# Recurrent half of an output projection by one Strassen step, with the bias tables moved to another pool and a plain block moved up in the attention half

## The chip, the cores and the metric

The kernel runs on one core of one Trainium2 chip. The metric is device time in microseconds (us) of one execution. TensorE is called PE, VectorE DVE, ScalarE ACT, GpSimd POOL and SyncE SP, as in the profile.

## The reference, cut to what matters

One layer of an encoder with 512 positions and model width 1024, in float32. The part around the change is this:

```python
y_rnn = (h_f + h_b) * gelu(gate)                    # (512, 512), recurrent heads
y_attn = dilated_attention(qh, kh, vh, rel_bias)    # (512, 512), 8 heads of 64
mix = concatenate([rms_norm(y_rnn, norm_rnn_g), rms_norm(y_attn, norm_attn_g)], axis=-1)
x = x + mix @ w_out                                 # w_out: (1024, 1024)
h = rms_norm(x, mlp_norm_g)
x = x + square(relu(h @ w_up)) @ w_down             # 1024 -> 4096 -> 1024
return rms_norm(x, final_norm_g)
```

The rows 0 to 511 of `w_out` belong to the recurrent half of `mix`, the rows 512 to 1023 to the attention half.

## The kernel before

Every matrix product is made in three fp32r passes (`mm3`, lines 311 to 314): each operand is split into a high part (rounded) and a low part (the rest), and high times high, high times low and low times high are added in PSUM. A weight block of 128x1024 comes by DMA into a buffer (`wraw`, three of them, or `tw`, four of them), ACT writes its high part (`conv_hi`, L260) and DVE its low part (`conv_lo`, L268). Blocks are numbered in the list `chunks`, and a block is split three blocks ahead of its use. When a plain block's low part is done, its buffer is free and the next plain block is asked for on SP's queue.

The order of work on PE, ACT, DVE and POOL is the order in which the program emits it. The order on SP, which only issues DMAs, is found by the framework's scheduler, which puts a load as early as its buffer allows.

The stages are these. First the columns of `w_in` for the recurrent input (tiles `pxr`), loaded together with the input in tiles `tw` and `wraw`. Behind them ACT splits the blocks 3, 4 and 5 one after the other (block 3 is from `w_in`, the blocks 4 and 5 are the first two of the value weights `w_v`), then copies the row of norm factors (`rrow`, L405). DVE takes these three blocks' low parts (L268) and then makes `xr` from `pxr` and `rrow` (L474, `conv_a`) and the convolution (L481 to 483). On PE follow the values (`pv`) and, after three steps of it, the first of four groups of gate matmuls (`pg`, L502). A group needs the convolution's first tile and the four PSUM banks that the four `pxr` tiles occupied, so it needs `xr` of all four.

Then the attention runs in five phases i = 0 to 4 of four units u each, written out in a loop. Phase i has the scores of head pair i (PE `pn`, `pf`; DVE L816, L797; ACT's exponentials L819), the transposes of the exponentials of pair i-1 (PE `pt`, L831, copied by ACT as `ett`, L833), and at its end the product with the values (`pav`, L912) of pair i-1. DVE makes `yp` from `pav` (L936), ACT squares it (`ysq`, L582) and scales it into `at` (L939). Between these pieces stand fillers, taken from a queue: 48 steps of the query and key projections (`pqk`) and then the steps of the recurrent half of the output projection (`wo_thunks`, `pwo`). A step is one `mm3`, three matmuls of 128x512. The table `plan` puts the small operations of ACT and DVE at (i, u, slot), and `FILL` says how many fillers a slot takes in the phases 3 and 4. When the projections are done, `load_x` loads the residual `x1` into the space of the normalised input, and the blocks and sums of `w_out` for the attention half into `ws`.

The recurrent half is plain: 4 row tiles of 128 times 2 column halves times 4 contraction tiles, 32 steps or 96 matmuls, out of four weight blocks. Its results are multiplied with the norm's factor and added to `x1` by DVE (L975), 8 times. The norm's gain is put in when ACT and DVE split `yrnn` (`y_hi`, `y_lo`).

After the last `pav` come five steps of it, the column sums of squares (`pcs`), nine more steps, and then the attention half (`wo_m`, `wo_x`), which is one Strassen step: seven products of half-size blocks, 28 steps, in the order of the table `OSEQ`. In Strassen's scheme in this form the product "11" lies in two PSUM banks (called "a" in the code, one for each of two row tiles), and "s2", "s3" and "s4" add to the same banks. After each of the four products DVE reads the banks and adds them to some tile of `x1` (L1141), and PE may go on in that bank only after that. The products "21" (banks "c") and "s1" with "22" (banks "b") have banks of their own. Each product's operands of the activations are sums (`osum`) split into `oh` (ACT) and `ol` (DVE).

Of the kernel before, what the change touches and what calls it, by code (L numbers as in the profile page):

```python
# [59 lines left out]
OSEQ = ("11", "s2", "s3", "s4", "21", "s1", "22")  # L60
# [48 lines left out]
def hybrid_kernel(ctx: ExitStack, tc, xw, xn, w_in, w_v, w_out, w_up, w_dn, gates, vecs, rel, onehot, fg, out):  # L109
# [22 lines left out]
    def f(t):  # L132
        return t.bitcast(FT)
# [64 lines left out]
    for n in range(2):  # L198
        for q in range(2):
            chunks.append(w_out[0, n, q])  # L200
    for n in OSEQ:
        chunks.append(("o", n))
# [14 lines left out]
    C_V, C_G, C_QK, C_WO, C_WA, C_UP = 4, 8, 12, 20, 24, 31  # L217
# [6 lines left out]
    def source(c):  # L224
        if not isinstance(c, tuple):
            return c
        if c[0] == "o":
            return oblock(c[1])
        return ublock(*c[:3]) if len(c) == 4 else wblock(*c)

    def oblock(b):
        return w_out[1, int(b[1]) - 1, int(b[0]) - 1]
# [6 lines left out]
    def emit_dma():  # L239
        if plain:  # L240
            i = plain.popleft()
            r = stream.tile([P, 1024], FT, name="wraw", tag="wraw", bufs=3)
            nc.sync.dma_start(r, source(chunks[i]))
            raws[i] = r
# [18 lines left out]
    def conv_lo(i):  # L263
        if i < len(chunks):
# [6 lines left out]
            if isinstance(c, tuple) and c[0] == "o":  # L271
                if c[1][0] != "s":
                    emit_dma()
            elif isinstance(c, tuple) and len(c) == 4:
# [300 lines left out]
    ycat = {}  # L575
# [16 lines left out]
    def y_hi(k, y):  # L592
        ycat[k] = (g_("yh", FR), g_("yl", FR))
        act(ycat[k][0], y, AF.Copy, scale=vec("yg", k))

    def y_lo(k, y):
        hi, lo = ycat[k]
        stt(lo, y, vec("yg", k), f(hi), op0=OP.mult, op1=OP.subtract)

# [5 lines left out]
    def rnn_cols():  # L605
        rc[0] = rstd_cols(col_sums(ssy[0], "et"), S)

# [349 lines left out]

    def wo_thunks():
        order = [(0, tt, k) for tt in range(4) for k in range(4)] + [(1, tt, k) for h in (0, 2) for tt in range(4) for k in (h, h + 1)]
        pw = {}  # L960

        def mk(b, n, tt, k):
            def run():
                if k == 0:
                    pw[n, tt] = ps_("pwo", "pj")
                o = pw[n, tt]
                hi, lo = splits[C_WO + 2 * n + k // 2]
                sl, tsl = slice((k % 2) * S, (k % 2 + 1) * S), slice(tt * P, (tt + 1) * P)
                mm3(o, [t[:, tsl] for t in ycat[k]], (hi[:, sl], lo[:, sl]), k == 0, k == 3)
                if b in (1, 17, 21, 25):  # L970
                    conv_hi(C_WO + {1: 3, 17: 4, 21: 5, 25: 6}[b])
                if b in (3, 19, 23, 26):
                    conv_lo(C_WO + {3: 3, 19: 4, 23: 5, 26: 6}[b])
                if k == 3:
                    stt(x1[tt, n], o, rc[0][:, tt:tt + 1], x1[tt, n], op0=OP.mult, op1=OP.add)  # L975
            return run
        return [mk(b, *o) for b, o in enumerate(order)]
# [17 lines left out]
    for p in range(1, 4):  # L995
        fillers.extend(q_thunks(p, 1) + q_thunks(p, 0))
    fillers.append(None)
    fillers.extend(wo_thunks())

    def load_x():  # L1000
        xb = big.tile([P, KD, S], FT, name="x1", tag="bigA")
        for n in range(2):
            for g in range(4):
                x1[g, n] = xb[:, 2 * g + n, :]
                nc.sync.dma_start(x1[g, n], xn[2 * g + n])
# [16 lines left out]
    def hi(t):  # L1022
        return lambda: y_hi(t, yrnn[t])

    def lo(t):
        return lambda: y_lo(t, yrnn.pop(t))
# [10 lines left out]
    def op(fn, *a):  # L1037
# [4 lines left out]
            (0, 1, 1): [sq_(1)],  # L1042
            (0, 2, 3): [add],
            (1, 0, 2): [end(2)],
            (1, 1, 0): [sq_(2)], (1, 1, 2): [end(3)], (1, 1, 4): [add],
            (1, 3, 0): [sq_(3)], (1, 3, 2): [hi(0)], (1, 3, 3): [add, hi(1)], (2, 0, 2): [rnn_cols],
            (2, 0, 0): [lo(0), lo(1)], (2, 0, 4): [hi(2)],
            (2, 1, 2): [hi(3)], (2, 1, 4): [lo(2)], (2, 2, 3): [lo(3)]}
# [19 lines left out]
    FILL = {(3, u): (0, 1, 1, 0) for u in range(4)}  # L1068
# [54 lines left out]
    OEND = {"11": (0, 0), "21": (0, 0), "s1": (1, 1), "22": (0, 1), "s2": (0, 1), "s3": (1, 1), "s4": (1, 0)}  # L1123
# [63 lines left out]
    for w in OSEQ:  # L1187
        for i in range(4):
            tt, k = i // 2, i % 2
            wo_m(w, tt, k)  # L1190
            if k == 1:
                wo_x(w, tt)
            if i in BES[w]:
                BES[w][i]()
        if w in ("s3", "s4", "21"):
            load_t(0, {"s3": "t1", "s4": "t2", "21": "t3"}[w], 4)
# [538 lines left out]
```

## Time and profile before

| | us |
|---|---|
| median of 3 runs | 535.03 (534.88 to 535.32) |
| the profiled execution | 534.21 |
| its span, first to last instruction | 532.3 |
| PE busy in the span | 523.7 |
| DVE busy in the span | 423.9 |
| ACT busy in the span | 352.6 |

The profile is of one execution, so a sum of durations is made against 534.21 us, of which 532.3 are the span. A row of the time line has the start, the duration, the engine, the line, the operation, the tile written and those read, the shape, the count, and in brackets how long the engine was idle before it and what ended that. PE's matmuls overlap: one of 128x512 is shown with 0.39 us, and the next starts earlier than that. A row "engine A <- engine B" of the table of waits counts the waits of A that B ended. A row of the table of stretches has, for each engine, the busy time and the number of instructions, then the granted clock of PE, the share of the DMA engines' time and the rate.

### The profile page before, as it was taken

The page shows a single profiled execution, that of the slowest core. Times are in us where ns is not written, and L with a number is a line of the kernel's source. Part 1 is how long each engine was busy: PE and PEld are TensorE (multiplying, and loading weights), DVE is VectorE, ACT ScalarE, POOL GpSimd, SP SyncE. Part 2 cuts the span into 40 slices and gives each one's busy share as a digit, 9 for nine tenths or more (in the row PEclk, how much of TensorE's full clock was granted, in tenths as well). Part 3 has the DMA queues.
Part 4 walks back from the last instruction along what each step waited for, and adds up shares of the span by engine and source line. Part 5 has one row for each costly group of instructions (what it writes and reads, how often), then busy time and mean ns, then how long its engine had stood idle before and what let it go on. Part 6 is the DMA issues. An engine that isn't in the chain of part 4 may idle for free.

```text
span 532.3 us, 9168 instructions
## 1 busy us (share of the span) xinstructions
PE 523.7 (98%) x3507; PEld 449.0 (84%) x3507; DVE 423.9 (80%) x695; ACT 352.6 (66%) x559; POOL 63.8 (12%) x90
## 2 busy tenths in 40 slices
PE   9999999999999999999999999999999999999994
PEld 7866888787877778899999888888999999888884
DVE  6897787786766788799779986879756987987885
ACT  7667958566858536586577755565567677655654
POOL 4330000000002210001110222001101200141000
PEclk9999999999999999999999999999999999999998
DMA  7754065384299788848495999985878496799604
GB/s 278 230 154 135 30 187 194 102 157 122 67 327 308 153 173 248 280 162 195 131 210 150 224 267 277 311 294 140 288 216 226 106 222 202 170 299 263 166 0 158
DMA packets 34587, 104.10 MB, mean 196 GB/s; under 512 B 3981, under 2 KB 6954, under 8 KB 34544
## 3 DMA queue, kind: packets, MB, share of 16 engines
q1 hardware_dynamic: 25712, 73.61, 40.5%
q0 software_dynamic: 7920, 28.61, 28.5%
q10 hardware_dynamic: 912, 1.30, 1.2%
q8 instruction: 27, 0.44, 0.3%
q14 instruction: 16, 0.13, 0.1%
HBM read 96.15 MB, written 4.21 MB: 189 GB/s over the span
## 4 chain that ended last, share of the span: by engine, by line
PE 96%; ACT 1%; DVE 1%; issue 0%; DVEq 0%; ACTq 0%
PE pu L313 10%; PE pu L312 10%; PE pu L314 10%; PE pd L312 9%; PE pd L314 9%; PE pd L313 9%; PE pqk L312 3%; PE pqk L314 3%; PE pqk L313 3%; PE pwo L312 2%; PE pwo L314 2%; PE pwo L313 2%; PE pt L831 2%; PE pg L502 2%; PE pav L912 2%; PE pv L312 2%
## 5 line engine op out<-in xcount | busy, mean ns | idle before, releaser
L268 DVE TENSOR_TENSOR wlo<-wraw,whi 128x1024 fp32r<-128x1024 f32 x73 | 88.9, 1220 | 23.9 <-ACT whi L260 23.0
L260 ACT ACTIVATE whi<-wraw 128x1024 fp32r<-128x1024 f32 x70 | 74.0, 1058 | 40.6 <-PE pd L314 20.4
L313 PE MATMUL pd<-wlo,ah 128*128 128x512 f32 (+1 forms) x195 | 75.2, 386 | 0.0
L312 PE MATMUL pd<-whi,ah 128*128 128x512 f32 (+1 forms) x195 | 75.2, 386 | 0.0
L314 PE MATMUL pd<-whi,al 128*128 128x512 f32 (+1 forms) x195 | 75.2, 386 | 0.0
L260 ACT ACTIVATE whi<-tw 128x1024 fp32r<-128x1024 f32 x36 | 38.1, 1061 | 38.6 <-PE pu L313 8.6
L313 PE MATMUL pu<-hl,whi 128*128 128x256 f32 x224 | 63.4, 283 | 0.0
L314 PE MATMUL pu<-hh,wlo 128*128 128x256 f32 x224 | 63.4, 283 | 0.0
L312 PE MATMUL pu<-hh,whi 128*128 128x256 f32 x224 | 63.4, 283 | 0.0
L312 PE MATMUL pu<-h2h,whi 128*128 128x256 f32 (+1 forms) x200 | 60.1, 300 | 0.0
L313 PE MATMUL pu<-h2l,whi 128*128 128x256 f32 (+1 forms) x200 | 60.0, 300 | 0.0
L314 PE MATMUL pu<-h2h,wlo 128*128 128x256 f32 (+1 forms) x200 | 60.0, 300 | 0.0
L268 DVE TENSOR_TENSOR wlo<-tw,whi 128x1024 fp32r<-128x1024 f32 x36 | 44.0, 1223 | 18.2 <-ACT whi L260 18.2
L312 PEld LDWEIGHTS pu<-hh,whi 128*128 128x128 f32 x224 | 43.0, 192 | 0.0
L313 PEld LDWEIGHTS pu<-hl,whi 128*128 128x128 f32 x224 | 43.0, 192 | 0.0
L314 PEld LDWEIGHTS pu<-hh,wlo 128*128 128x128 f32 x224 | 43.0, 192 | 0.0
L314 PEld LDWEIGHTS pd<-whi,al 128*128 128x128 f32 x195 | 36.6, 188 | 7.4
L313 PEld LDWEIGHTS pd<-wlo,ah 128*128 128x128 f32 x195 | 36.6, 188 | 7.4
L312 PEld LDWEIGHTS pd<-whi,ah 128*128 128x128 f32 x195 | 36.6, 188 | 7.3
L260 ACT ACTIVATE whi<-ts 128x1024 fp32r<-128x1024 f32 x24 | 25.5, 1061 | 24.3 <-PE pd L314 18.4
L312 PEld LDWEIGHTS pu<-h2h,whi 128*128 128x128 f32 x200 | 38.3, 191 | 1.3
L314 PEld LDWEIGHTS pu<-h2h,wlo 128*128 128x128 f32 x200 | 38.3, 191 | 1.3
(268 smaller groups left out, 1223.9 us busy)
## 6 DMA issues: line engine op xcount, KB each, us to landing
wraw<-in_w_up_dram SPq DMA_DIRECT2D x25, 512.0 KB
ts<-in_w_dn_dram POOLq DMA_DIRECT2D x24, 512.0 KB, 13.3
wraw<-in_w_dn_dram SPq DMA_DIRECT2D x24, 512.0 KB
tw<-in_w_up_dram SPq DMA_DIRECT2D x15, 512.0 KB
tw<-in_w_up_dram POOLq DMA_DIRECT2D x15, 512.0 KB, 8.3
wraw<-in_w_in_dram SPq DMA_DIRECT2D x13, 512.0 KB
ts<-in_w_dn_dram SPq DMA_DIRECT2D x8, 512.0 KB
tw<-in_w_dn_dram SPq DMA_DIRECT2D x8, 512.0 KB
```

The lines of the kernel that those rows point to most:

```text
L260: act(hi, raws[i], AF.Copy)
L268: nc.vector.tensor_tensor(lo, r, f(splits[i][0]), op=OP.subtract)
L312: nc.tensor.matmul(o, lhsT=a[0], rhs=b[0], start=bool(first), stop=False, skip_group_check=on)
L313: nc.tensor.matmul(o, lhsT=a[0], rhs=b[1], start=False, stop=False, skip_group_check=on)
L314: nc.tensor.matmul(o, lhsT=a[1], rhs=b[0], start=False, stop=bool(last), skip_group_check=on)
L502: nc.tensor.matmul(pg[2 * d + j][halves[b ^ d]], lhsT=gwr[t][halves[b], c], rhs=xc[t][halves[b]], start=True, stop=True)
L831: nc.tensor.transpose(pt[:, i * P:(i + 1) * P], en[h][u][:, c * P:(c + 1) * P], ident)
L912: nc.tensor.matmul(o(half[e]), lhsT=v[:, h * DH:(h + 1) * DH], rhs=c(et[h, x]), start=first, stop=last, skip_group_check=True)
```

## The change

1. The recurrent half is made by the same Strassen step as the attention half: 7 products of 4 steps, so 28 steps or 84 matmuls, in the order `RSEQ`. Each step is an `mm3` of the same shape. DVE reads PSUM and adds to `x1` 14 times (line 1013 of the changed kernel), two after each product, and "s2", "s3" and "s4" again go on in the banks of "11".
2. The weights of the recurrent half are seven blocks: "11", "21" and "22" as they are, and the four sums "s2", "s3", "s1", "s4". The sums are made by DMA in `tw` tiles: a plain load on SP's queue (`load_r`) and one or two accumulating loads on POOL's; the sum "s4" is the buffer of "s2" with one more block added, once "s2" is split.
3. The activations get four sums on DVE (`r_sum`, 8 operations of 128x256), seven splits (`r_hi` on ACT, `r_lo` on DVE) in place of four, and the gain is put in by a copy on ACT (`scaled`), four times.
4. The bias tables of the attention (`load_tw`) are tiles of the general pool "g" in place of `tw` tiles. Four of the eight tiles of `x1` are in that pool too and are loaded earlier (`first_x`).
5. The first three steps of the recurrent half stand between the last three of the query projection. In phase 3 a unit takes 3 fillers in place of 2; so 22 steps are done before the last `pav` in place of 18. After it come five, the column sums, and one more in place of nine.
6. In the attention half "21" moves from the fifth place to the second.

The core of the diff:

```diff
-OSEQ = ("11", "s2", "s3", "s4", "21", "s1", "22")
+OSEQ = ("11", "21", "s2", "s3", "s4", "s1", "22")
+RSEQ = ("11", "s2", "s3", "s4", "s1", "21", "22")
...
-        t = work.tile([P, 1024], FT, name="tw", tag="tw", bufs=4)
+        t = g_("tb")
...
+    def r_sum(n):
+        o = rsb[n] = g_("rsum")
+        for k in range(2):
+            c = slice(k * TH, (k + 1) * TH)
+            a, b = yrnn[k], yrnn[k + 2]
+            if n == "s1":
+                nc.vector.tensor_tensor(o[:, c], b[:, tr], a[:, tr], op=OP.subtract)
...
     def wo_thunks():
-        order = [(0, tt, k) for tt in range(4) for k in range(4)] + [(1, tt, k) for h in (0, 2) for tt in range(4) for k in (h, h + 1)]
         pw = {}
-        def mk(b, n, tt, k):
+        def mk(j, w, tt, k):
+            b = {"21": "c", "s1": "b", "22": "b"}.get(w, "a")
+            new = w in ("11", "21", "s1")
             def run():
...
+                mm3(o, r_part(w, tt, k), (hi[:, sl], lo[:, sl]), k == 0 and new, k == 1, True)
+                m = 2 * tt + k
+                if m == 1:
+                    conv_hi(C_WO + j + 3)
+                if m == 3:
+                    conv_lo(C_WO + j + 3)
+                if k == 1:
+                    i, n = OEND[w]
+                    g = 2 * i + tt
+                    stt(x1[g, n], o, rc[2 if n else 0][:, g:g + 1], x1[g, n], op0=OP.mult, op1=OP.add)
...
+    def load_r(w, bs):
+        t = work.tile([P, 1024], FT, name="tw", tag="tw", bufs=4)
+        nc.sync.dma_start(t, oblock(bs[0], 0))
+        for b in bs[1:]:
+            nc.gpsimd.dma_start(t, oblock(b, 0), accum_op=OP.add)
+        raws[C_WO + RSEQ.index(w)] = t
...
+    wt = wo_thunks()
+    for n in (5, 3, 1):
+        fillers.insert(len(fillers) - n // 2, wt.pop(0))
     fillers.append(None)
-    fillers.extend(wo_thunks())
+    fillers.extend(wt)
...
-    FILL = {(3, u): (0, 1, 1, 0) for u in range(4)}
+    FILL = {(3, u): (1, 1, 1, 0) for u in range(4)}
```

Two places of the order are shown. The first is SP's queue at the start of the program. `xw` is the input with the first weights, `gwr` are the gate weights, `w_v` the value weights; `tw_1109` and `tw_1159` are the sums "s2" and "s3" of the recurrent half. Before:

```order
L336 DMA tw_124<-in_xw_dram 128x896
L243 DMA wraw_210<-in_w_in_dram 128x1024
L243 DMA wraw_220<-in_w_v_dram 128x1024
L243 DMA wraw_223<-in_w_v_dram 128x1024
L320 DMA gwr_212<-in_gates_dram 128x256
L320 DMA gwr_214<-in_gates_dram 128x256
L320 DMA gwr_216<-in_gates_dram 128x256
L320 DMA gwr_218<-in_gates_dram 128x256
L243 DMA wraw_323<-in_w_v_dram 128x1024
L243 DMA wraw_327<-in_w_v_dram 128x1024
```

And SP's queue at the same place after the change:

```order
L337 DMA tw_124<-in_xw_dram 128x896
L1023 DMA tw_1109<-in_w_out_dram 128x1024
L241 DMA wraw_210<-in_w_in_dram 128x1024
L241 DMA wraw_220<-in_w_v_dram 128x1024
L1023 DMA tw_1159<-in_w_out_dram 128x1024
L321 DMA gwr_212<-in_gates_dram 128x256
L321 DMA gwr_214<-in_gates_dram 128x256
L321 DMA gwr_216<-in_gates_dram 128x256
L321 DMA gwr_218<-in_gates_dram 128x256
L241 DMA wraw_223<-in_w_v_dram 128x1024
L241 DMA wraw_323<-in_w_v_dram 128x1024
L241 DMA wraw_327<-in_w_v_dram 128x1024
```

Two loads of 512 KB for the recurrent half's sums now stand among the first loads, and the second value block (`wraw_223`, block 5) has moved behind one of them and behind the four gate loads.

The second place is DVE's row of work after the last `yp`, where the column sums end and the attention half begins. `ol` are low parts of the activations' sums, `wlo` those of weight blocks, `rc1` and `nrc` the norm's factors; L975 before and L1013 after read the recurrent half's PSUM, L1141 before and L1191 after that of the attention half. Before:

```order
L881 TENSOR_TENSOR ol_2144<-at_2140,oh_2143 128x512
L268 TENSOR_TENSOR wlo_2158<-wraw_1443,whi_2112 128x1024
L1171 RECIPROCAL rc1_2180<-rc1_2180 128x4
L1173 TENSOR_SCALAR nrc_2183<-rc1_2180 128x4
L875 TENSOR_TENSOR ol_2070<-osum_2051,oh_2069 128x256
L268 TENSOR_TENSOR wlo_2190<-ws_1714,whi_2169 128x1024
L975 SCALAR_TENSOR_TENSOR x1_1705<-pwo_2105,rcol_1_1579,x1_1705 128x512
L268 TENSOR_TENSOR wlo_2204<-ws_1714,whi_2198 128x1024
L975 SCALAR_TENSOR_TENSOR x1_1705<-pwo_2151,rcol_1_1579,x1_1705 128x512
L975 SCALAR_TENSOR_TENSOR x1_1705<-pwo_2162,rcol_1_1579,x1_1705 128x512
L975 SCALAR_TENSOR_TENSOR x1_1705<-pwo_2171,rcol_1_1579,x1_1705 128x512
```

And DVE's row at the same place after the change:

```order
L875 TENSOR_TENSOR ol_2226<-at_2222,oh_2225 128x512
L266 TENSOR_TENSOR wlo_2240<-wraw_1985,whi_2193 128x1024
L1013 SCALAR_TENSOR_TENSOR x1_1466<-pwr_2233,rcol_1_1607,x1_1466 128x512
L1013 SCALAR_TENSOR_TENSOR x1_1468<-pwr_2061,nrc0_1609,x1_1468 128x512
L1221 RECIPROCAL rc1_2262<-rc1_2262 128x4
L1223 TENSOR_SCALAR nrc_2265<-rc1_2262 128x4
L869 TENSOR_TENSOR ol_2147<-osum_2128,oh_2146 128x256
L266 TENSOR_TENSOR wlo_2272<-ws_1769,whi_2251 128x1024
L1013 SCALAR_TENSOR_TENSOR x1_1470<-pwr_2119,nrc0_1609,x1_1470 128x512
L869 TENSOR_TENSOR ol_2184<-osum_2126,oh_2183 128x256
L1191 SCALAR_TENSOR_TENSOR x1_1464<-pwo_2277,rc1_2262,x1_1464 128x512
L869 TENSOR_TENSOR ol_2198<-osum_2130,oh_2197 128x256
```

Three readings of the recurrent half (L1013) now stand in this stretch, and the first reading of the attention half (L1191) follows the third of them; one weight split (L268) and three readings that stood between have gone from it. Behind these rows stand, after the change, a reading of "11", a weight split, the two readings of "21", a weight split, and then the first reading of "s2".

More of the change, by code (lines that the diff above doesn't have):

```diff
@@ L573, in scan_ops_end @@
         return both
-    ycat = {}
     ssy = {}
@@ L977, in wo_thunks @@
-        return [mk(b, *o) for b, o in enumerate(order)]
+                if new and k == 0:
+                    pw[b, tt] = ps_("pwr", "pj")
+                o = pw[b, tt]
+                hi, lo = splits[C_WO + j]
+                sl = slice(k * S, (k + 1) * S)
+                mm3(o, r_part(w, tt, k), (hi[:, sl], lo[:, sl]), k == 0 and new, k == 1, True)
[4 more added lines that the diff above has]
+                    conv_lo(C_WO + j + 3)
```

106 lines of the change are left out of this document (59 added, 47 removed).

## The prediction

> **What bounds the kernel now.** I read the page first, then the table of PE's waits, then the time line at the places where the change touches the order. The page and the waits say that PE is the bound everywhere:
>
> ```profile
> span 532.3 us, 9168 instructions
> PE 523.7 (98%) x3507; PEld 449.0 (84%) x3507; DVE 423.9 (80%) x695; ACT 352.6 (66%) x559; POOL 63.8 (12%) x90
> PE pwarm L154 <- DVE epsb L145: 1.0, 1, 1.0
> PE pt L831 <- ACT ett L833: 0.6, 1, 0.6
> PE pav L912 <- ACT ett L833: 0.2, 1, 0.2
> ```
>
> PE is busy for 98% of the span, and the three rows of waits are all that it has: one at the start of the program, and two at the end of the attention, where the transposes and the last `pav` wait for ACT's copies. So a matmul taken away is time won, and a wait added on PE is time lost in full. Work added to DVE and ACT costs nothing where those run ahead of PE, and all that it holds PE up where they don't. The question is at which places they are just in time already.
>
> **The matmuls that go.** The rate of PE in this stage is read from the first matmul of two steps in a row:
>
> ```profile
> 187.08 0.39 PE L312 MATMUL pwo<-whi,oh 128*128 128x512 f32 x1
> 187.76 0.39 PE L312 MATMUL pwo<-whi,oh 128*128 128x512 f32 x1
> ```
>
> A step is 187.76 - 187.08 = 0.68 us, its three matmuls 0.227 us each. Four steps go (32 to 28): 4 x 0.68 = 2.72 us. This term is firm, since the new steps have the same shape.
>
> **The loads at the start.** Two loads of 512 KB now stand among the first ones, and the second value block (block 5) comes behind one of them and behind the gate weights.
>
> ```profile
> 13.04 0.33 SPq L243 DMA_DIRECT2D wraw<-in_w_in_dram  x1
> 14.77 2.06 SPq L243 DMA_DIRECT2D wraw<-in_w_v_dram  x2
> 16.89 1.85 SPq L320 DMA_DIRECT2D gwr<-in_gates_dram  x4
> 14.00:22.00 8.00, 8.00 (x41) 6.76 (x40) 6.61 (x12) 4.93 (x8) 0.90 (x1) 1.00 0.84 258
> 12.00:13.00 1.00, 1.00 (x6) 0.84 (x5) 1.00 (x3) 1.00 (x3) 0.00 (x0) 1.00 0.06 22
> 22.06 1.06 ACT L260 ACTIVATE whi<-wraw 128x1024 fp32r<-128x1024 f32 x1 [1.97 <-DMA wraw<-in_w_v_dram]
> 24.17 0.60 ACT L405 ACTIVATE rrow<-prow 128x512 f32<-128x512 f32 x1 [1.05 <-PE prow L391]
> 20.93 3.50 DVE L268 TENSOR_TENSOR wlo<-wraw,whi 128x1024 fp32r<-128x1024 f32 x3
> 24.81 1.29 DVE L474 TENSOR_TENSOR xr<-pxr,rrow 128x512 f32<-128x512 f32 x2 [0.38 <-ACT rrow L405]
> 31.45 0.68 DVE L474 TENSOR_TENSOR xr<-pxr,rrow 128x512 f32<-128x512 f32 x1
> 30.90 2.37 PE L502 MATMUL pg<-xc,gwr 64*64 64x512 f32 x16
> 40.04 1.95 PE L502 MATMUL pg<-xc,gwr 64*64 64x512 f32 x16
> ```
>
> The first of the two loads ("s2") needs a buffer that the second input tile leaves early, so it goes into the lull at 12 to 13 us (22 GB/s) and costs nothing. The other ("s3") has its buffer too and is issued between the value blocks. From 14 to 22 us the DMA engines moved 258 GB/s x 8 us = 2.06 MB, which is the `w_in` block, two value blocks and the gates. One more block of 0.524 MB takes 0.524 / 0.258 = 2.0 us. ACT already waits for block 5 until 22.06 us. If block 5 shares the engines with the gates, as its late landing in the row suggests (its load was issued before the gates', and yet it came when nearly all of their bytes had moved), it is 2.0 us later; if the gates, as many bytes, now stand wholly ahead of it, 4.1 us. Against that, the engines were busy for only 0.84 of these 8 us, and the new load may fill part of the rest, down to a delay of about 0.4 us.
>
> What hangs on it: ACT's `rrow` stands behind this split in ACT's row, and DVE's `xr` behind block 5's low part. DVE ended its three low parts at 20.93 + 3.50 = 24.43 us and began `xr` at 24.81, so 0.38 us of the delay is hidden. From there to the fourth `xr` (31.45 to 32.13 us) DVE works with hardly a pause, and the first gate group on PE needs that fourth `xr` for its last bank: it takes 2.37 us, where the third takes 1.95, so PE waits there already. All the rest of the delay is therefore PE's. I take a delay of 2.4 us, nearer to the sharing, and 2.4 - 0.38 = **+2.0 us** (bounds 0 and 3.7). The Trainium skill's page "DMA: Bandwidth & Descriptors", section "Queues, rings and completion order", says that each DMA engine consumes the descriptors of one ring in the order in which they were put there. By that rule the upper case would hold, and the term would be 3.7 us. The late landing at 22.06 us speaks for less order than that, unless a few engines lag behind the others.
>
> The other loads that move forward ("s1", the first sum for the MLP) are issued behind all value blocks, and the accumulating ones on POOL behind the bias tables; what they push back is read by DVE much later:
>
> ```profile
> 39.52 0.22 DVE L439 CAST relr<-relt 97x128 fp32r<-97x128 f32 x1
> 42.45 0.68 DVE L510 TENSOR_TENSOR ga<-ga,xcs 128x512 f32<-128x512 f32 x1
> ```
>
> So I cost them at nothing; if that cover were gone, at most one load's 2.0 us more.
>
> **The phases of the attention.** In phases 1 and 2 the sums and splits are added, and cost nothing if DVE and ACT catch up before the next phase; DVE waits for PE there still, and ACT too:
>
> ```profile
> 131.04 1.10 DVE L936 TENSOR_TENSOR yp<-pav,zrow 128x512 f32<-128x512 f32 x1 [1.86 <-PE pav L912]
> 142.64 0.48 DVE L816 CUSTOM_DVE_ANT_0 e<-pn,tw,mf 128x256 f32<-128x256 f32 x1 [2.08 <-PE pn L777]
> 132.18 0.63 ACT L582 ACTIVATE ysq<-yp 128x512 f32<-128x512 f32 x1 [3.63 <-DVE yp L936]
> ```
>
> In phase 1 DVE gets three sums and a low part, some 2.5 us, ahead of a wait of 1.86 us and an earlier one; without that cover about 1 us would be open. In the last two units of phase 3 it is tighter. DVE gets two more readings of PSUM (0.66 us apart), a weight split (1.14 us from one start to the next) and two low parts (0.60 us): 3.7 us, while PE gets two more steps, 1.36 us.
>
> ```profile
> 162.13 0.75 DVE L975 SCALAR_TENSOR_TENSOR x<-pwo,rcol,x 128x512 f32<-128x512 f32 x1 [1.46 <-PE pwo L314]
> 163.40 2.82 PE L912 MATMUL pav<-ett,vs 128*64 128x128 f32 x32
> 168.11 0.63 ACT L582 ACTIVATE ysq<-yp 128x512 f32<-128x512 f32 x1 [0.17 <-DVE rz L842]
> 170.50 1.14 PE L831 MATMUL pt<-ident,e 128*128 128x128 f32 x8 [0.56 <-ACT ett L833]
> 173.24 3.30 PE L912 MATMUL pav<-ett,vs 128*64 128x128 f32 x32 [0.20 <-ACT ett L833]
> ```
>
> DVE's wait of 1.46 us takes some of it: 3.7 - 1.36 - 1.46 = 0.9 us by which `yp` and ACT's `ysq` are later against PE. ACT's copies `ett` stand behind `ysq`, and PE waits for them (0.56 and 0.20 us). ACT also gets a weight split (1.06 us) ahead of the first of these copies. I take **+0.5 us** (bounds 0, and 0.9 + 1.06 = 1.9).
>
> **From the last `pav` to the attention half.** Here four steps that PE had after the column sums are done earlier, and four more are gone, so that PE comes to the attention half eight steps sooner. DVE does not. The rows from the last `yp` on:
>
> ```profile
> 176.58 1.11 DVE L936 TENSOR_TENSOR yp<-pav,zrow 128x512 f32<-128x512 f32 x1 [0.89 <-PE pav L912]
> 180.27 0.68 DVE L881 TENSOR_TENSOR ol<-at,oh 128x512 fp32r<-128x512 f32 x1
> 180.87 1.22 DVE L268 TENSOR_TENSOR wlo<-wraw,whi 128x1024 fp32r<-128x1024 f32 x1
> 182.01 0.17 DVE L1171 RECIPROCAL rc<-rc 128x4 f32<-128x4 f32 x1
> 182.29 0.42 DVE L875 TENSOR_TENSOR ol<-osum,oh 128x256 fp32r<-128x256 f32 x1
> 182.62 1.21 DVE L268 TENSOR_TENSOR wlo<-ws,whi 128x1024 fp32r<-128x1024 f32 x1
> 183.76 0.74 DVE L975 SCALAR_TENSOR_TENSOR x<-pwo,rcol,x 128x512 f32<-128x512 f32 x1
> 184.42 1.21 DVE L268 TENSOR_TENSOR wlo<-ws,whi 128x1024 fp32r<-128x1024 f32 x1
> 191.80 0.74 DVE L1141 SCALAR_TENSOR_TENSOR x<-pwo,nrc,x 128x512 f32<-128x512 f32 x1
> 180.01 0.95 PE L411 MATMUL pcs<-ones,ysq 128*128 128x1 f32 x8
> 192.69 0.47 PE L312 MATMUL pwo<-whi,oh 128*128 128x512 f32 x1
> ```
>
> Count from the start of `yp`, at 176.58 us. DVE is done with `ol` at 180.87, 4.29 us later, and that part is not changed. From one start to the next a weight split takes 182.01 - 180.87 = 1.14 us, a reading of PSUM 184.42 - 183.76 = 0.66, a small `ol` 182.62 - 182.29 = 0.33, and the two small operations on the norm's factor 0.28 together. After the change DVE has to do, up to the end of the first reading of "s2": four weight splits (4.56), seven readings and the one that ends (7 x 0.66 + 0.74 = 5.36), the small ones (0.28) and three `ol` (0.99), 11.2 us. So that reading ends 4.29 + 11.2 = 15.5 us after `yp`. PE must wait for it before "s3" goes on in that bank. PE's own way there is five steps and the column sums, over at 180.01 + 0.95 = 180.96 (4.4 us after `yp`), one step, and twelve steps of "11", "21" and "s2": 4.4 + 13 x 0.68 = 13.2 us. PE waits **15.5 - 13.2 = 2.3 us**. "21" in second place takes the wait from the start of "s2" to the start of "s3", but does not shorten DVE's row. Before, the same reading ended at 192.54 us, 16.0 after `yp`, and PE's step there began at 192.69, some 0.17 us late against its beat; that goes. So DVE is ahead of PE by nothing at this place before as well, and PE's eight steps only turn into a wait. After "s3" a product is 2.72 us on PE and 1.14 + 2 x 0.66 = 2.5 us on DVE, so the lag goes and nothing more is lost. Bounds: 1.0 (if DVE gains on the pieces ahead of `ol`) and 3.1 (one more reading ahead).
>
> **The sum**, against the profiled execution: -2.72 + 2.0 + 0.5 + 2.3 - 0.17 = +1.9 us, a span of 534.2 and 536.1 us for the execution. The median of the runs lies 535.03 - 534.21 = 0.8 us above the profiled one, so I give 536.9 us.
>
> **The rivals.**
>
> *The start costs nothing*: the new load fits into the idle time of the DMA engines and block 5 comes before 22.06 + 0.38 us. For it: 0.84 busy, and the lull before. Against: block 5 is issued after more bytes. The sum is then -0.1, 534.9 us, not slower. Chance 0.11.
>
> *DVE's row at the attention half does not hold PE*: it decides at 13.2 us after `yp`. For it: some pieces of DVE's row wait for ACT and could shorten together. Against: it held PE in the row at 192.69 already. Then -2.72 + 2.0 + 0.5 - 0.17 = -0.4 us, 534.6 us. Chance 0.09.
>
> *Both*: -2.4 us, 532.6 us, down to the whole gain at 532.3. Chance 0.22, more than the product, since one error in how I read the queues would undo both terms.
>
> *Ring order at the start*: 2.0 becomes 3.7 us, 538.6 us. Chance 0.10.
>
> *More waits in the phases*: each step of "s2", "s3" and "s4" needs DVE's reading of the same bank two steps before, and between these readings stand scores and splits. If DVE lags by 1 us at each of the three, 3 us more, 539.9 us. Chance 0.08.
>
> **How the numbers follow.** My forecast has 0.40, at 536.9 us, and by its bounds 535.5 to 539. A measurement here tells 0.2%, 1.1 us, from no change. Slower by more than that: 0.40 + 0.10 + 0.08 = 0.58. The same: 0.11 + 0.09 = 0.20. Faster: 0.22. The range goes from 532.9, which leaves out about half of the case of both gains, to 540.0.
>
> **What would show it.** Right: PE's first gate group some 2 us later and longer than 2.37 us; ACT's third weight split later than 22.06 us; a wait of PE for DVE's reading of some 2 us at the start of "s3" in the attention half, and no other of that size. Wrong: the first gate group at 30.9 us as before, or the attention half without a wait on PE, which then ends some 5 us sooner after the last `pav` than before.

## The result, and the profile after

The changed kernel takes 544.11 us (median of 4 runs, 543.97 to 544.71) against 535.17 us of the kernel before beside it (534.88 to 535.32): ratio 1.017, 95% interval 1.0152 to 1.0187. The forecast was slower, 536.9 us, at most 540.0. So the sign was right, and 7 us of the loss were not in the sum.

The page of after, its first lines:

```profile
span 542.3 us, 9189 instructions
PE 525.3 (97%) x3495; PEld 448.2 (83%) x3495; DVE 434.9 (80%) x717; ACT 358.8 (66%) x570; POOL 66.3 (12%) x95
```

Its table of PE's waits (us in total, times, longest):

```profile
PE prow L392 <- ACT ett L827: 5.8, 1, 5.8
PE pwo L313 <- DVE x L1191: 1.9, 1, 1.9
...
```

The second row is the forecast wait in the attention half. The first, three times as long, stands in phase 1 of the attention, where the prediction had none. To see what each stretch lost, take the same instruction in both traces. Before, at the fourth gate group, at the scores of phases 1 and 2, and at the last transposes:

```profile
44.18 1.95 PE L502 MATMUL pg<-xc,gwr 64*64 64x512 f32 x16
111.04 0.99 PE L777 MATMUL pn<-kraw,qraw 64*32 64x192 f32 x32
130.93 0.99 PE L777 MATMUL pn<-kraw,qraw 64*32 64x192 f32 x32
210.30 1.91 PE L1151 MATMUL pxt<-ident,x1n 128*128 128x128 f32 x16
```

After, the same four, with ACT's third weight split (before at 22.06), the first gate group (30.90), the column sums behind the last `pav` (180.01) and the first step of the attention half (187.08):

```profile
24.22 1.06 ACT L258 ACTIVATE whi<-wraw 128x1024 fp32r<-128x1024 f32 x1 [3.68 <-DMA wraw<-in_w_v_dram]
31.82 3.12 PE L503 MATMUL pg<-xc,gwr 64*64 64x512 f32 x16
45.92 1.95 PE L503 MATMUL pg<-xc,gwr 64*64 64x512 f32 x16
112.78 0.99 PE L771 MATMUL pn<-kraw,qraw 64*32 64x192 f32 x32
141.22 0.99 PE L771 MATMUL pn<-kraw,qraw 64*32 64x192 f32 x32
193.45 0.95 PE L412 MATMUL pcs<-ones,ysq 128*128 128x1 f32 x8
195.05 0.40 PE L313 MATMUL pwo<-whi,oh 128*128 128x512 f32 x1
220.53 1.91 PE L1201 MATMUL pxt<-ident,x1n 128*128 128x128 f32 x16
```

After stands 1.74 us behind at the fourth gate group and at the scores of phase 1 (112.78 - 111.04), 10.29 at those of phase 2, 7.97 at the attention half, 10.23 at the last transposes, and 10.0 at the end. The stretches so cost +1.7 (start), **+8.6 (phase 1)**, 7.97 - 10.29 = -2.3 (phases 2 to 4 with the recurrent half: -2.72 for the four steps, +0.4), +2.3 (attention half), and -0.2 (rest).

Phase 1 is read from SP's rows (`tb` are the loads of the bias tables), two of DVE and three of PE:

```profile
97.75 0.55 SPq L464 DMA_DIRECT2D tb<-nbd  x1
108.38 0.33 SPq L241 DMA_DIRECT2D wraw<-in_w_out_dram  x1
108.76 0.53 SPq L463 DMA_DIRECT2D tb<-nbd  x1
107.13 1.22 DVE L266 TENSOR_TENSOR wlo<-wraw,whi 128x1024 fp32r<-128x1024 f32 x1
122.14 0.29 DVE L791 CUSTOM_DVE_ANT_0 e<-pf,tb 128x128 f32<-128x128 f32 x1 [7.03 <-DMA tb<-nbd]
126.54 1.12 PE L392 MATMUL prow<-ident,rzb 128*128 128x128 f32 x4 [5.80 <-ACT ett L827]
128.74 0.63 PE L313 MATMUL pqk<-h_hi,whi 128*128 128x512 f32 x1
129.16 0.63 PE L314 MATMUL pqk<-h_lo,whi 128*128 128x512 f32 x1
```

SP's queue holds the table of head 3 behind a weight block. That block waits for its buffer, until DVE's low part (107.13 to 108.35) has read it, and SP issues nothing between 98.30 and 108.38. The table goes out at 108.76 and is there at 122.1; DVE waits 7.03 us, ACT's exponentials and copies wait for DVE, and PE for ACT. Before, the tables had the ring of four big buffers, and those of phase 1 (the rows are their near parts) went out some 40 us ahead of use:

```profile
66.84 0.57 SPq L462 DMA_DIRECT2D tw<-nbd  x1
72.94 0.55 SPq L462 DMA_DIRECT2D tw<-nbd  x1
112.99 0.29 DVE L797 CUSTOM_DVE_ANT_0 e<-pf,tw 128x128 f32<-128x128 f32 x1 [2.19 <-PE pf L784]
```

The 5.8 us idle don't end the loss. Windows of after (PE, PEld, DVE, ACT, POOL busy; then PE's granted clock, the DMA engines' share, GB/s):

```profile
122.00:126.00 4.00, 0.00 (x0) 0.00 (x0) 3.79 (x17) 2.75 (x7) 0.00 (x0) 0.91 0.27 91
126.00:131.00 5.00, 4.46 (x26) 3.03 (x34) 4.77 (x19) 4.75 (x11) 0.00 (x0) 0.50 0.10 32
```

From 126 to 131 us the clock is 0.50, and matmuls start 129.16 - 128.74 = 0.42 us apart in place of 0.227. That is the rest of the 8.6: 2.8 us. The Trainium skill's page "TensorE: Matmul & The Clock Gate", section "What's actually happening", has half rate after an idle window of about 3.4 us and full rate after about 3.4 us of sustained work. The rows agree in that half rate follows these 5.8 us idle, and that full rate comes back under work, here after some 5 us; own_ring, below, has half rate behind 1.93 us idle too, and there the measurement decides.

### The profile page after: what moved, and what is told of

Read it like the earlier page. It is cut to its first block, busy times and chain, and to the rows that moved or that the text cites. A ratio compares the mean times of both kernels' runs of the same rounds, so it can differ in the third digit from the quotient of the medians.

```text
span 542.3 us, 9189 instructions
## 1 busy us (share of the span) xinstructions
PE 525.3 (97%) x3495; PEld 448.2 (83%) x3495; DVE 434.9 (80%) x717; ACT 358.8 (66%) x570; POOL 66.3 (12%) x95
## 4 chain that ended last, share of the span: by engine, by line
PE 80%; DVE 9%; DMA 4%; ACT 4%; issue 2%; SPq 0%; DVEq 0%; ACTq 0%
PE pu L313 10%; PE pu L315 10%; PE pu L314 10%; PE pd L314 9%; PE pd L315 9%; PE pd L313 9%; DMA tb<-nbd 2%; PE pqk L313 2%; PE pqk L315 2%; PE pqk L314 2%; PE pav L906 2%; PE pv L313 1%; PE pp L314 1%; PE pp L313 1%; PE pp L315 1%
## 5 line engine op out<-in xcount | busy, mean ns | idle before, releaser
L258 ACT ACTIVATE whi<-wraw 128x1024 fp32r<-128x1024 f32 x69 | 72.9, 1058 | 39.5 <-PE pd L315 19.3
L258 ACT ACTIVATE whi<-tw 128x1024 fp32r<-128x1024 f32 x40 | 42.3, 1059 | 36.7 <-DMA tw<-in_w_up_dram 10.4
L266 DVE TENSOR_TENSOR wlo<-tw,whi 128x1024 fp32r<-128x1024 f32 x40 | 48.9, 1223 | 16.8 <-ACT whi L258 16.8
L258 ACT ACTIVATE whi<-ts 128x1024 fp32r<-128x1024 f32 x24 | 25.5, 1062 | 26.4 <-PE pd L315 18.2
L314 PEld LDWEIGHTS pu<-h2l,whi 128*128 128x128 f32 x200 | 38.3, 192 | 1.3
```

Of the source, the lines that this page charges most:

```text
L258: act(hi, raws[i], AF.Copy)
L266: nc.vector.tensor_tensor(lo, r, f(splits[i][0]), op=OP.subtract)
L314: nc.tensor.matmul(o, lhsT=a[0], rhs=b[1], start=False, stop=False, skip_group_check=on)
```

## The experiments

Theory **tables**: the 8.6 us come from the tables' place on SP's queue. Rivals: the buffer comes free late; DVE lags anyway through the added sums; the transfer is slow by itself.

**own_ring**: tables in four buffers of their own.

```diff
-        t = g_("tb")
+        t = work.tile([P, 480], FT, name="tb", tag="tb", bufs=4)
...
-    NG = 48
+    NG = 44
```

> The changed kernel with the bias tables in a ring of four buffers of their own (the general ring of 512-column tiles has 44 in place of 48); nothing else differs. Theory (tables): 5.8 us of PE's idle time and some 2.5 us of half clock behind it come from the second pair of tables, which now gets a general buffer late, stands on SP's queue behind a weight block that waits for DVE, and lands at 122 us. With buffers of their own the tables of heads 2 and 3 are loaded some 40 us ahead of their use: the wait and the clock drop go, 544.1 - 8.4 = 535.7 us. Rival (DVE): the table wait only covers a lag that DVE and ACT have in phases 1 and 2 anyway from the added sums; then under half of it comes back, 540 us or more.

536.25 us (10 runs, 534.31 to 537.48); ratio to before 1.0021 (1.0007 to 1.0035). The wait is gone, and with it nearly all of the excess: from the scores of phase 1 to those of phase 2 PE takes 19.89 us before, 28.44 after and 19.87 in own_ring. DVE's lag is no cause in phase 1. The profile keeps the wait of 1.93 us at "s3", and the window behind it shows that the clock can fall there too:

```profile
198.00:201.00 3.00, 3.00 (x8) 2.34 (x8) 1.48 (x2) 0.00 (x0) 0.00 (x0) 0.50 0.23 44
```

Three of its runs take 534.3 to 534.8 us at a mean clock of 0.997 or 0.998, seven 535.7 to 537.5, six of them at 0.994 or 0.995. The profiles say what the drop costs. Seven of them, after and six experiments, have this wait, of 1.91 to 1.95 us. In four (own_ring, tables_split, sums_late, sum_behind) the clock falls behind it, and from the first step of the attention half to the last transposes PE takes 27.0 to 27.1 us; in three (after, tables_pool, tables_early) it doesn't, and PE takes 25.4 to 25.5. So the drop costs 1.6 us and doesn't always come.

**before_tables_only**: the kernel before, with the one edit `t = g_("tb")`.

> The kernel before with one edit: the bias tables in general work tiles, as in the change; no Strassen step in the recurrent half, the old order of the attention half. Theory (tables): the wait of some 6 us and the clock drop show here too, and as the four big buffers that the tables leave are free from the start, the first loads for the MLP are issued among the first value blocks and cost the start-up what it costs after the change (1.7 us): 535.2 + 8.4 + 1.7 = 545.3 us. Rival (the step's own loads and sums make the tables late): 535 to 537 us.

542.64 us, ratio 1.0152 (1.0135 to 1.0169), with the same wait and no Strassen step:

```profile
PE prow L391 <- ACT ett L833: 5.1, 1, 5.1
```

So the tables' move alone, which the prediction never priced, costs 7.7 us, with what it does to the start. It is 2.7 less than expected: the scores of phase 2 stand at 139.42 us here, 8.5 behind, of which 1.9 are from the start (fourth gate group 46.11), so 6.6 are the tables', with a shorter stretch at low clock than after.

**tables_pool**: general buffers, but issued by POOL (`nc.gpsimd.dma_start` in place of `nc.sync`).

> The changed kernel with the loads of the tables issued by POOL in place of SP, at the same places in the program and from the same general ring. Theory (place on the queue): POOL isn't held by a weight block that waits for DVE, so the tables of head 3 go out when their buffer is free, well before 108.8 us, and land before 112.8: 535.7 us, up to 1 us more for POOL's accumulating loads, which wait in between. Rival (buffer): the buffer itself comes free as late as that, and the wait stays: 542 to 544 us. Rival (transfer): the table is slow because four DMA engines carry it, and an earlier issue helps only by the time gained.

537.05 us (7 runs), ratio 1.0044 (1.0026 to 1.0063); no wait for a table. POOL's rows:

```profile
68.75 0.68 POOL L463 DMA_DIRECT2D tb<-nbd  x1
78.76 1.03 POOL L463 DMA_DIRECT2D tb<-nbd  x1
```

The tables of phases 0 and 1 are all out by 80 us (head 2 at 68.75, head 3 at 78.76), in the same general ring. So the buffer was free, and SP's order, behind weight blocks that wait for DVE, was the cause. The statement further up that the scheduler puts a load as early as its buffer allows does not hold for these tables; why it put them where they stand, no run shows.

**tables_early**: asked for one phase earlier, still on SP.

```diff
             load_tw(1)
+            load_tw(2)
+            load_tw(3)
...
-                if i < 3:
-                    load_tw(2 * i + 2 + u // 2)
+                if i < 2:
+                    load_tw(2 * i + 4 + u // 2)
```

> The changed kernel with the tables left in the general ring of 48, but asked for one phase earlier in the program (heads 0 to 3 together, then two phases ahead of use). Theory (tables): 535.7 us as with a ring of their own, since only the place on SP's queue and the time of landing matter. Rival (general ring): the tables hold buffers of the general ring for longer and something else waits for one; over 538 us. Rival (DVE): 540 us or more.

540.54 us (538.52 to 542.84), the time of the two rivals, but the way of neither. The tables' wait is gone, but four tables in a row now hold SP and the DMA engines, and the block of the input projection behind them is late (ACT splits it at 84.16, after at 77.84); PE then waits in phase 0:

```profile
69.09 2.12 SPq L463 DMA_DIRECT2D tb<-nbd  x1
84.16 1.06 ACT L258 ACTIVATE whi<-wraw 128x1024 fp32r<-128x1024 f32 x1 [10.53 <-DMA wraw<-in_w_in_dram]
101.47 1.09 PE L773 MATMUL pn<-kraw,qraw 64*32 64x192 f32 x32 [2.71 <-DVE qraw L745]
```

**tables_split**: the changed kernel, each table in eight transfers.

```diff
+        for c in range(4):
+            r = slice(32 * c, 32 * c + 32)
-        nc.sync.dma_start(near, bass.AP(tensor=nbd.tensor, offset=o, ap=[[1, 4], [4, 32], [1, 2 * P]]))
+            nc.sync.dma_start(near[r], bass.AP(tensor=nbd.tensor, offset=o + c, ap=[[4, 32], [1, 2 * P]]))
...
```

> The changed kernel with each table loaded by eight transfers of 32 partitions in place of two of 128; same buffers, same place on SP's queue. With only tables under way the DMA engines were 0.27 busy at some 90 GB/s, as if four of the sixteen carried them. Theory (transfer): the smaller transfers spread over more engines; the second table lands some 5 us sooner although SP takes longer to issue it, PE's wait falls from 5.8 to 1 to 2 us and with it the clock drop: 537 to 539 us. Rival (place on the queue alone): issued behind the same weight block at 108.8 us and eight issues long, it lands no sooner: 544 us or more.

539.8 us (4 runs, 538.73 to 542.75), between the two, nearer to the transfer. The table of head 3 still goes out behind the weight block, from 107.45 us on. That is 4.0 us ahead of the scores of phase 1 (111.47), as after (112.78). Yet DVE reads it 3.1 us behind them, at 114.53, where after it was 9.4, at 122.14; PE's waits there are 1.9 and 1.1 us, behind ACT:

```profile
107.06 0.35 SPq L241 DMA_DIRECT2D wraw<-in_w_out_dram  x1
107.45 0.46 SPq L465 DMA_DIRECT2D tb<-nbd  x1
114.53 0.29 DVE L793 CUSTOM_DVE_ANT_0 e<-pf,tb 128x128 f32<-128x128 f32 x1 [0.72 <-PE pt L827]
119.07 1.15 PE L827 MATMUL pt<-ident,e 128*128 128x128 f32 x8 [1.91 <-ACT ett L829]
```

So the slow transfer was the other half of the loss: phase 1 is 3.8 us longer than before, in place of 8.6. In the window 122 to 126 us of after the DMA engines are 0.27 busy at 91 GB/s: 0.27 x 16 = 4.3 engines. The Trainium skill's page "DMA: Bandwidth & Descriptors", section "Why a DMA increments its semaphore by 16 and not by 1", says that a transfer uses the largest number of engines, up to 16, that divides the slowest dimension of both access patterns. That is 4 in `[[1, 4], [4, 32], ...]`; the share agrees. The 32 of the split form would give 16; how many it used, no window shows.

**The start.** The theory puts the 1.7 us on the second sum ("s3") between the value blocks; a rival, on the first input tile, whose split came at 6.83 us after and 5.92 before.

**sums_late**: own_ring, all sums' loads behind a small copy from the split relative table (39.5 us); the first MLP load likewise. **sum_behind**: "s3" and "s1" alone, behind one from the norm's factor, some 24 us; the first MLP load as in sums_late.

```diff
+        nc.gpsimd.tensor_copy(t[0:NB3, :1], f(relr)[:, :1])
         nc.sync.dma_start(t, oblock(bs[0], 0))
```

```diff
+        if w != "s2":
+            nc.gpsimd.tensor_copy(rt[w][:, :1], rcol[:, :1])
         nc.sync.dma_start(rt[w], oblock(b, 0))
```

> own_ring with the loads of the recurrent sums (and the first one for the MLP) held back until the relative table is split on DVE (39.5 us), so that SP issues them behind all value blocks; the sums are the same. Theory (start): two of these loads, 512 KB each, ahead of the second value block put ACT's third weight split from 22.06 to 24.2 us, and PE's gate groups 1.7 us back. Then the split is at 22.1 us again, the fourth gate group at 44.2 in place of 45.9, and the time 536.25 - 1.7 = 534.5 us. Rival (late first tile): the lag comes from the first input tile, which also landed up to 0.9 us later; then the split stays near 24 us and the time over 535.5. Rival (contention): the loads now fall on the blocks of the input projection between 40 and 80 us, and as much is lost there.

> own_ring with the second of the early sums (s3) and the third (s1) held back until POOL has the norm's factor of the input, about 24 us: the first sum stays in the lull at 9 us, the second comes behind the gate weights and the second value block. Theory (start): the delay of 1.7 us at the start belongs to the one load between the value blocks. ACT's third split is back near 22 us, the fourth gate group within 0.5 us of 44.2, and, with the loads of the input projection left where they were, no new wait at 100 us: 536.3 - 1.4 = 534.9 us. Rival (any place costs): as in sums_late a block of the input projection or a value block now comes late and PE waits for it: 536 us or more.

sums_late: 542.39 us (4 runs), ratio 1.0138 (1.0123 to 1.0153). The start is mended, and the rival on contention then came: an input-projection block is late, and PE waits 3.84 us for the scores.

```profile
21.30 1.06 ACT L258 ACTIVATE whi<-wraw 128x1024 fp32r<-128x1024 f32 x1 [0.96 <-DMA wraw<-in_w_v_dram]
44.56 1.95 PE L513 MATMUL pg<-xc,gwr 64*64 64x512 f32 x16
82.40 1.06 ACT L258 ACTIVATE whi<-wraw 128x1024 fp32r<-128x1024 f32 x1 [10.09 <-DMA wraw<-in_w_in_dram]
101.22 1.09 PE L781 MATMUL pn<-kraw,qraw 64*32 64x192 f32 x32 [3.84 <-DVE qraw L753]
```

sum_behind: 534.95 us (12 runs), ratio 1.0004 (0.9993 to 1.0014), without a new wait at 100 us; ACT's third split is at 22.56. The median is 1.3 us under own_ring's, but the two intervals overlap. The runs with a mean clock of 0.996 or more take 534.4 to 535.0 us here (7) and 534.3 to 535.8 in own_ring (4), the others 535.9 to 536.6 (5) and 535.9 to 537.5 (6). So the medians differ mostly because fewer runs here have the low clock, and a gain in time from the load's place is not shown.

**before_again**: the kernel before, profiled once more.

> The kernel before once more, profiled. Theory (chance at the start): the first input tile's landing varies from run to run by up to 1.3 us, as in the kernels above (6.06 to 7.25 us), and was early, 5.92, in the profile that the prediction read; each microsecond of it moves the fourth gate group by as much. Then its group stands at 44.18 plus what the tile is later. Rival (the change makes it late): the tile lands at 5.9 us again and the group stands at 44.2.

The tile's split came at 6.38 us (0.46 later) and the fourth gate group at 44.76 (0.58 later), 534.9 us. Against the first profile of before (first fence: the tile's split), sum_behind, without the load between the blocks, has both 1.33 to 1.34 us late. own_ring, with the load, has the tile only 0.32 late and the group 1.74 late, as after (third fence):

```profile
5.92 0.72 ACT L342 ACTIVATE h_hi<-tw,vt 128x512 fp32r<-128x512 f32 x1 [0.68 <-DMA tw<-in_xw_dram]
```

```profile
7.25 0.72 ACT L343 ACTIVATE h_hi<-tw,vt 128x512 fp32r<-128x512 f32 x1 [1.97 <-DMA tw<-in_xw_dram]
45.52 1.95 PE L503 MATMUL pg<-xc,gwr 64*64 64x512 f32 x16
```

```profile
6.24 0.72 ACT L343 ACTIVATE h_hi<-tw,vt 128x512 fp32r<-128x512 f32 x1 [1.03 <-DMA tw<-in_xw_dram]
24.31 1.06 ACT L258 ACTIVATE whi<-wraw 128x1024 fp32r<-128x1024 f32 x1 [3.55 <-DMA wraw<-in_w_v_dram]
45.92 1.95 PE L503 MATMUL pg<-xc,gwr 64*64 64x512 f32 x16
```

So the first tile's landing differs from profile to profile (5.92 and 6.38 us for the same kernel), and where the load is absent, in seven profiles, the group is as late as the tile to within 0.25 us. Where it is present, the two don't add: the group needs `xr`, and `xr` comes behind the later of the two (in after DVE waits 1.09 us for the third split ahead of it, in sum_behind 0.38 for `rrow`). In own_ring the tile is nearly on time and the load alone gives the whole 1.74 us; in after, whose tile is 0.91 late, it gives the same. All ten profiles that have a load there (before_tables_only has one for the MLP) agree: the split comes 0.95 to 2.83 us late, and the group is late by the split's delay less 0.42 to 0.52 us, 0.4 to 2.3 us, whatever the tile does. So the theory was right for after; its 1.74 us is one draw of that scatter.

**The attention half.**

**old_order**: own_ring, `OSEQ` as before.

> own_ring with the attention half in its old order (11, s2, s3, s4, 21, s1, 22). Theory (DVE's row): the second plain block in second place only takes PE's wait for DVE's readings from the start of s2 to the start of s3; with the old order the wait stands at s2, of 2 to 3.5 us, and the time is within 1.5 us above own_ring (536.3 to 537.8). Rival (a product of slack): the block moved up gives DVE a whole product, 2.7 us, more; then the old order costs 2.7 us, 539 us.

536.43 us (12 runs), ratio 1.0020 (1.0008 to 1.0031): the same as own_ring. PE waits 2.4 us at the start of "s2" in place of 1.9 at "s3", so moving "21" forward is worth nearly nothing, as DVE's row says.

```profile
PE pwo L313 <- DVE x L1191: 2.4, 1, 2.4
```

**s1_between**, **s1_between_b**: own_ring, "s1" between "s2" and "s3".

```diff
-OSEQ = ("11", "21", "s2", "s3", "s4", "s1", "22")
+OSEQ = ("11", "21", "s2", "s1", "s3", "s4", "22")
```

> own_ring with s1 of the attention half taken out of the end and put between s2 and s3, with the transposes of the output's first half behind s4 (order 11, 21, s2, s1, s3, s4, 22). Theory (bank): PE's 1.9 us at the start of s3 is the wait for DVE's reading of the bank that s2 left; s1 goes into another bank, so PE has 2.7 us of work there while DVE catches up. The wait falls to 0.5 us or less, and the drop of the granted clock that followed it in own_ring (0.98 from 200 to 220 us) goes too: 534.0 to 534.6 us. Rival (throughput): DVE has more work than PE over the whole half, and the wait only turns up later, at s4 or at the transposes: 535.5 us or more.

> s1_between again, with s3 in place of s1 as the product that ends the sum of the second half's columns; the order on PE is the same (11, 21, s2, s1, s3, s4, 22). Theory (bank): as s1_between measured, 534.8 us, 1.5 us under own_ring: no wait at the start of s3, one of about 1.4 us at the transposes, where DVE's last readings of s4 end. Rival: what the earlier one gained came from the order of the sums: 536 us.

534.8 and 535.34 us (12 and 11 runs). The first leaves the product "s1" out of one quarter of the output's sums; the second has it. The wait at "s3" is gone, and one of 1.4 us stands at "s4" in both: the bank was right as the place, the rival on throughput right as the reason. From the first step of the half to the last transposes PE takes 25.5 us in both, as after; what is gained on own_ring's profile (27.1) is the drop of the clock, which none of these profiles has behind the shorter wait. From s1_between_b:

```profile
PE pwo L313 <- DVE x1n L1191: 1.4, 1, 1.4
```

**lows_on_pool**: some low parts on POOL.

```diff
-        nc.vector.tensor_tensor(osp[k][1], at[2 + k], f(osp[k][0]), op=OP.subtract)
+        (nc.gpsimd if k else nc.vector).tensor_tensor(osp[k][1], at[2 + k], f(osp[k][0]), op=OP.subtract)
...
```

> own_ring with the low parts of the second half of the attention's sums, and of its plain half, made by POOL in place of DVE: in the stretch behind the last pav one operation of 128x512 and three of 128x256, some 1.6 us of DVE's row, of which 1.3 stand ahead of the reading that PE waits for. Theory (DVE's row): PE's wait at the start of s3 falls from 1.9 to some 0.7 us, 535.0 us. Rival (POOL is slow, or slows DVE beside it): PE waits for POOL's low part in place of DVE's reading, 537 us or more.

536.71 us (9 runs), ratio 1.0034 (1.0023 to 1.0045): nothing gained. The rival was right that POOL is slow and slows DVE, though not in what PE waits for: that is 1.29 us for DVE's reading of the recurrent half and 1.25 for an ACT weight split later. The 128x512 takes 1.32 us on POOL and 0.68 on DVE, and DVE's weight split beside POOL 1.76 in place of 1.22:

```profile
187.09 3.28 POOL L869 TENSOR_TENSOR ol<-osum,oh 128x256 fp32r<-128x256 f32 x3
187.34 1.76 DVE L266 TENSOR_TENSOR wlo<-wraw,whi 128x1024 fp32r<-128x1024 f32 x1
```

**both**: own_ring with sum_behind's and s1_between_b's edits. **both_less**: the same without two of DVE's weight splits. **before_less**: the kernel before without them.

```diff
-            nc.vector.tensor_tensor(lo, r, f(splits[i][0]), op=OP.subtract)
+            if c in (("o", "s1"), ("o", "s3")):
+                lo = splits[i][0]
+            else:
+                nc.vector.tensor_tensor(lo, r, f(splits[i][0]), op=OP.subtract)
```

> sum_behind and s1_between_b in one kernel. Theory (the terms add): 536.3 - 1.4 - 1.5 = 533.4 us, 1.6 us under the kernel before, of the 2.7 us that the four steps fewer are worth on PE. Rival (DVE bound): what the start gives is lost again at the transposes; 534.5 us or more.

> both, with two operations of DVE left out in the attention half: the low parts of the weight blocks s3 and s1 aren't made, and the high parts stand in for them, so PE has the same matmuls and the output lacks these blocks' low bits. Theory (DVE): from the last pav on, DVE's row has more work than PE's steps since the step, and the 1.4 us that PE waits at s4 in both are its lag. Two weight splits are 2 x 1.14 = 2.3 us: the wait goes, and the small one at the first matmul of the MLP may go too: 534.7 - 1.7 = 533.0 us. Rival (ACT, or the order of the banks): the wait stays above 1 us, 534.3 us or more.

> The control: the kernel before with the same two operations of DVE left out. Theory (DVE): before the step DVE's reading came only 0.17 us late, and PE had no wait in the half, so it gains 0.2 us at most: 534.9 to 535.3. Rival (it bound it already): DVE held PE before as well, in waits that the profile doesn't show; 534.2 us or less.

both: 534.71 us (11 runs), ratio 0.9992 (0.9983 to 1.0001), the lowest median of a complete form, 9.4 us under the change as it was, and no different from the kernel before. both_less: 533.6 us (7 runs, 532.75 to 536.5). before_less: 534.74 against 534.77. The 1.1 us between both and both_less are not clear of the scatter: two of the seven runs take over 536 us, at a clock of 0.993. The traces are. In both_less PE's wait at "s4" is gone, and PE takes 24.10 us from the first step of the half to the last transposes, where the kernel both takes 25.51 (its first step and transposes, then those of both_less):

```profile
185.44 0.40 PE L313 MATMUL pwo<-whi,oh 128*128 128x512 f32 x1
210.95 1.91 PE L1208 MATMUL pxt<-ident,x1n 128*128 128x128 f32 x16
```

```profile
185.13 0.40 PE L316 MATMUL pwo<-whi,oh 128*128 128x512 f32 x1
209.23 1.91 PE L1211 MATMUL pxt<-ident,x1n 128*128 128x128 f32 x16
```

Before, the same stretch takes 23.22 us, in before_less 23.23. So the two operations are worth 1.4 us with the step and nothing without it: DVE holds PE in the attention half since the step. Of the 2.3 us that the kernel both takes more than before there, 0.9 stay open. The windows of before and of both from 160 to 180 us say where DVE got its work (PE, PEld, DVE busy):

```profile
160.00:180.00 20.00, 19.18 (x138) 14.63 (x137) 12.81 (x32) 15.39 (x34) 4.05 (x5) 1.00 1.01 269
```

```profile
160.00:180.00 20.00, 18.91 (x167) 13.97 (x165) 19.12 (x48) 17.51 (x38) 4.10 (x6) 1.00 0.82 179
```

## Why the prediction was right or wrong

- **The four steps, -2.72**: right. From the column sums to the attention half PE takes 7.07 us before and 1.60 after, 5.47 for the eight steps that it no longer makes there, 0.68 each. Four of them are done earlier, four are gone.
- **The start, +2.0**: right in its place (third split at 24.22, first gate group 3.12 us long), in its way and nearly in its size. The split is 2.16 us late where 2.4 was taken, 0.42 of it hidden where 0.38 was taken, and 1.74 us are left. With a scatter of 0.4 to 2.3 us between kernels, coming this near is partly luck. The price of strict ring order (3.7) didn't come in any of the ten profiles; whether the engines keep the order of a ring, they don't show.
- **The phases, +0.5**: 0.4 measured, where it was put. From the scores of phase 3 to the last `pav` PE takes 21.51 us before and 24.66 after, 3.15 more, of which four more steps are 2.72. The rival with more waits there didn't come.
- **The attention half, +2.3 - 0.17**: 2.3 measured, with 1.9 us of wait at "s3", where it was put. PE goes on there at 205.64 us, 15.6 after `yp` (190.02); 15.5 was computed. That DVE's row causes it is shown by both_less against before_less, for the wait where it stands in the kernel both.
- **What failed** is a term that isn't in the sum: the tables' change of pool, point 4 of the change, was put at nothing without a reason. The sentence "what they push back is read by DVE much later ... So I cost them at nothing" spoke of the sums' loads only, and where the tables' own loads would stand wasn't followed. In the old pool they went out 40 us ahead of use, in the general one they stand on SP in phase 0, behind a block that waits for DVE. The term is +8.6 us: 5.8 idle, 2.8 at half clock. The prediction's own test, a wait at "s3" "and no other of that size", is what failed in the trace.
- With that term, 536.9 + 8.6 = 545.5 against 544.1. Of the rest, 0.8 is what the prediction added because the profiled execution of before lay under its median; after's lies at its median. The start accounts for 0.3.
- The sign was not owed to the tables alone: own_ring, without that term, is still slower than before (ratio 1.0007 to 1.0035) and near the forecast with 536.25 us. That nearness has luck in it, since in its profile a drop of the clock that no term of the sum has adds 1.6 us.

## What to carry to other kernels

When a tile changes its pool, look where its load now stands on the issuing queue, what the entry ahead of it waits for, and how long before its use it goes out; a load that was free for being early has a price as soon as it is late. Price a saved matmul against the engine that must read its result: here 2.7 us fewer on PE became DVE's lag, since Strassen's form gives DVE more readings of PSUM, sums and low parts for fewer products. Before a difference of a microsecond is put down to an edit, compare the same stretch of both traces: here the clock and the first loads alone move a run by that much.

## What was unexpected of the hardware

A wait on PE can cost more than its length: 5.8 us were followed by some 5 us at a clock of 0.50, and even 1.93 us by 3 us at 0.50 in own_ring's profile, though not in after's own, where the clock is 1.00 behind the same wait. Of seven profiles with that wait four have the drop; the three with a wait of 1.4 us don't. A table of 240 KB took 13 us beside other loads from issue to use, in a form that some four DMA engines carry, and 7 us at most in smaller pieces. What decides whether the clock falls behind a short wait was not tried.
